# Gate, up and down of a feed-forward layer: the two products of neighbouring blocks in the order high, low, low, high

## The chip, the cores and the metric

The kernel runs on one core of a Trainium2 chip. The metric is the device time of one execution in microseconds (us), as the median of several runs. An execution under the hardware profiler gives the trace from which the rows in this document are copied.

## The reference

The program is the trunk of a streaming encoder: four layers on an input of 256 tokens by 1024 channels. Each layer has a token mixer (RWKV-7 time mixing in layers 0 and 3, stick-breaking attention in layer 1, attention over selected keys in layer 2) and a feed-forward part, each behind an RMS norm and with a residual add. The part that matters here is the feed-forward one:

```python
D_MODEL, SEQ, DEPTH = 1024, 256, 4
D_FF = -(-8 * D_MODEL // (3 * 256)) * 256      # 2816

def swiglu(h, w_gu, w_down):
    g, u = jnp.split(h @ w_gu, 2, axis=-1)
    return (jax.nn.silu(g) * u) @ w_down
...
        x = x + y
        x = x + swiglu(rms_norm(x, norm_ffn[i]), ffn_w_gu[i], ffn_w_down[i])
```

All is float32.

## The kernel before

**Data.** Channels lie on the 128 partitions, tokens along the free dimension. The residual stream is in four tiles `xt[j]`, each with two blocks of 128 channels by 256 tokens. A product needs a float32 result, but TensorE takes its operands in the format float32r at one pass. So each operand is split into a high part (the value rounded to float32r) and a low part (the value less the high part). A product of two split operands is made of three: high by high, high by low, low by high.

**The long and the short product.** For an activation block the high and the low part stand side by side in one tile, 512 columns. With the high weights loaded, one matmul over all 512 columns makes high by high in columns 0 to 255 of a PSUM bank and high by low in columns 256 to 511. With the low weights loaded, a second matmul over the first 256 columns adds low by high to columns 0 to 255. These two, called the high and the low product below, belong to one block of 128 input channels. Each needs its own weight load, a row LDWEIGHTS of engine PEld in the profile. The two halves of the bank are added later, by ScalarE's copy of columns 256 to 511 and VectorE's addition of columns 0 to 255 (`add2`, line 903).

**Weights.** `piece` (line 858) fetches 128x1024 float32 of weights by one DMA issued on SyncE into a tile `raw` (three buffers). The high part is made by a cast (`wh`, ScalarE as a rule), the low part by VectorE's subtraction (`wl`). There are three buffers of each. In gate and up every second piece uses three more pairs in the tile `wring`. A piece holds eight blocks of 128x128.

**Gate and up.** `ffn` (line 1019) runs over 11 groups of 256 channels. In each it makes two gate products and two up products by `gemm1` (line 908): eight blocks, each a unit of a high and a low product, summed in one bank. The moving tile is `xg`, the scaled input. ScalarE writes its high part block by block, VectorE its low part (`prep_chunk`, line 950). Then come scaling, SiLU, the product of gate and up, and the split of the result into `h`, high and low side by side. `gemm1` is also what layer 1's attention uses for its queries and keys (tile `qk`).

**Down.** For each of eight blocks of output channels, 22 blocks of `h` are summed in one bank `dn`, each again as a unit of a high and a low product; a piece covers eight blocks. VectorE then adds the bank to `xt`.

**What sets the order.** All operations are first recorded, and a planner (`Plan`) then orders them by a model of costs and due times, engine by engine. A unit (`with unit()`) is one entry for it: its matmuls stay together, in the order in which they were recorded. Units of different products may be mixed, save where `in_turn` keeps gate and up, or down, in their order. The instructions are all issued by one line of `emit`, so the profile shows nearly all of them as L779, and operations are told apart by their tiles.

**Other places of this trace that the prediction uses.** `vps` are layer 1's (and layer 2's) values: there the activations are loaded as weights, and the split weights move, 512 columns at a time, in the order high, low, high. `po` are the output projections, `qi` layer 2's index queries and `qk` layer 1's and 2's queries and keys. In `po`, `qi` and layer 2's `qk`, 256 columns move at a time, and the weights are in turn high, high, low. `warm_o` are products of constant data that keep TensorE busy.

Of the kernel before, what the change touches and what calls it, by code (L numbers as in the profile page):

```python
# [23 lines left out]
S = 256  # L24
D = 1024
NC = D // P
NF = 11
# [268 lines left out]
class Plan:  # L296
# [15 lines left out]
    def unit(self, at_once=1, ns=0.0):  # L312

        plan = self

        class Unit:
            def __enter__(self):
                plan.unit_op = Op("tensor")
                plan.unit_op.ns = ns

            def __exit__(self, *_):
                op, plan.unit_op = plan.unit_op, None
                op.cost /= at_once
                op.cost = op.ns or op.cost
                plan._add(op)

        return Unit()
# [63 lines left out]
    def after(self, op, preds):  # L391
        op.preds |= set(preds)
# [390 lines left out]
def trunk(ctx: ExitStack, tc: tile.TileContext, xT_in, vecs_in, wts, lora_in, consts_in, id32_in, outT, order, layers=None):  # L783
# [7 lines left out]
    pe, dve, act, pool, sp = (plan.queue(n) for n in ("tensor", "vector", "scalar", "gpsimd", "sync"))  # L791
# [3 lines left out]
    def T(shape, group=None, name="t", dtype=F32):  # L795
        return plan.tile(sb, [P] + list(shape), dtype, group, name)
# [7 lines left out]
    def bank(name, group="ps"):  # L804
        return plan.tile(psum, [P, 512], F32, group, name, "psum")
# [48 lines left out]
    def f(ap):  # L854
        return ap.bitcast(F32)


    def piece(key, raw=None, parts=None):

        i = len(order)  # L860
        order.append(key)
        r = T([PIECE], "raw", f"raw{i}") if raw is None else raw
        sp.dma_start(r, wts[i])
        h, l = (T([PIECE], "wh", f"wh{i}", F32R), T([PIECE], "wl", f"wl{i}", F32R)) if parts is None else parts
        anye.copy(h, r)
        dve.tensor_tensor(l, r, f(h), op=ALU.subtract)
        return h, l
# [26 lines left out]
    def v3(t, n):  # L894
        return t.rearrange("p (k m) -> p k m", k=n)
# [4 lines left out]
    def flat(t):  # L900
        return t.rearrange("p a b -> p (a b)")

    def add2(t, o, eng=anye):

        eng.copy(t, o[:, S:])
        dve.tensor_tensor(t, o[:, :S], t, op=ALU.add)

    def gemm1(key, x, name, group="g", raw=None, parts=None):


        out = bank(name, group)
        wh, wl = [v3(t, NC) for t in piece(key, raw, parts)]
        for c in range(NC):
            with unit():
                pe.matmul(out, wh[:, c], flat(x[:, c]), start=(c == 0), stop=False)
                pe.matmul(out[:, :S], wl[:, c], x[:, c, 0], start=False, stop=(c == NC - 1))
        return out

    def gemm2(key, xs, name):
# [76 lines left out]
    def rstd_bcast(summed=False):  # L996
        if summed:
            ss = nstate["ss"]
        else:
            ss, sq = bank("ss"), t1("ssq")  # L1000
            anye.tensor_tensor(sq, nstate["acc"][:, 0], nstate["acc"][:, 1], op=ALU.add)
            exact(ss[:, :S], onesr, sq, [T([S], "t", "ssr", F32R) for _ in range(2)])
        return rsqrt_of(ss[:, :S], S, "rstd", 1.0 / D, eps_rms)
# [15 lines left out]
    def ffn(layer, after):  # L1019
        x = nstate["xg"]  # L1020
        rsb = None
        hs = [v.rearrange("p (i k a s) -> p i k a s", i=n, k=2, a=2)
              for v, n in ((T([4096], g, "h", F32R), 4) for g in ("SA", "SZ", "PR"))]

        ring = T([6, PIECE], "QC", "wring", F32R)

        def place(n):

            return {"parts": (ring[:, n // 2 % 3], ring[:, 3 + n // 2 % 3]) if n % 2 else None}

        for i in range(NF):
            gus = T([2, 2, S], f"s{6 + i % 2}", "gus")
            gs, us = gus[:, 0], gus[:, 1]
            since = len(plan.ops)
            for k in range(2):
                add2(gs[:, k], gemm1(("g", layer, 2 * i + k), x, "gate", **place(4 * i + k)), act if i >= 0 else anye)
            if i == 0:
                rsb = rstd_bcast()[:, None, :].to_broadcast([P, 2, S])
            dve.tensor_tensor(gs, gs, rsb, op=ALU.mult)
            act.activation(gs, gs, AF.Silu)  # L1040
            for k in range(2):
                add2(us[:, k], gemm1(("u", layer, 2 * i + k), x, "up", "ps", **place(4 * i + 2 + k)), act if i >= 0 else anye)
            if i >= 1:
                plan.in_turn(since, "gate", "up")
            dve.tensor_tensor(us, us, rsb, op=ALU.mult)
            dve.tensor_tensor(us, us, gs, op=ALU.mult)
            h = hs[i // 4][:, i % 4]
            act.copy(h[:, :, 0], us)
            dve.tensor_tensor(h[:, :, 1], us, f(h[:, :, 0]), op=ALU.subtract)

        n, since = 0, len(plan.ops)
        for m in range(NC):
            o = bank("dn", "g" if m % 2 else "ps")
            for k in range(2 * NF):
                if n % NC == 0:
                    wh, wl = [v3(t, NC) for t in piece(("d", layer, n // NC))]
                h = hs[k // 8][:, k // 2 % 4, k % 2]
                with unit():
                    pe.matmul(o, wh[:, n % NC], flat(h), start=(k == 0), stop=False)
                    pe.matmul(o[:, :S], wl[:, n % NC], h[:, 0], start=False, stop=(k == 2 * NF - 1))  # L1060
                n += 1
            for a in range(2):
                dve.tensor_tensor(xt[m // 2][:, m % 2], xt[m // 2][:, m % 2], o[:, a * S:(a + 1) * S], op=ALU.add)
            if m == NC - 1:
                plan.in_turn(since, "dn")
            if m % 2:
                after(m // 2)
# [500 lines left out]
    def stick(layer, after):  # L1568
# [12 lines left out]
        for p in range(8):  # L1581
            q, k = qk_[:, p, 0], qk_[:, p, 1]
            add2(q, gemm1(("sq", p), x, "qk"))
            add2(k, gemm1(("sk", p), x, "qk"))
            if p == 0:
# [377 lines left out]
```

## Time and profile before

| | us |
|---|---|
| median of 3 runs | 1396.13 |
| lowest and highest of these | 1396.02, 1396.16 |
| the profiled execution | 1397.01 |
| its span, first to last instruction | 1395.1 |

In layer 0 the feed-forward part's gate and up run from 193.6 to 318.7 us of the span, and its down from there to 379.7.

In the profile PE is TensorE's matmuls, PEld its weight loads, DVE VectorE, ACT ScalarE, POOL GpSimd and SP SyncE. A group's row has the line, the engine, the operation, output and input tiles, the shapes and the count; then the busy time in us and the mean of one in ns; then the time for which the engine was idle ahead of them, and what ended it. A row in order of time has the start in us, the length in us from the first start to the last end, and then the same names. Rows of equal names that follow each other are merged, with their count. A row of a stretch has the stretch, its length, TensorE's busy time with the count of instructions, the granted clock, the share of DMA and GB/s. Ends of matmuls are modelled, and a record is longer than the time for which it holds the engine.

### The profile page before, as it was taken

The numbers are of one execution on the slowest core, as the hardware profiler recorded it, in microseconds if no ns is written. First come the engines' busy times: TensorE is split into PE (matmuls) and PEld (weight loads), VectorE is DVE, ScalarE is ACT, GpSimd is POOL, SyncE is SP. The second block draws the span as 40 slices with busy tenths as digits, with TensorE's granted clock in tenths as the row PEclk, the third lists the DMA queues.
The fourth block names the chain that finished last, engine by engine and source line by source line (L and its number), as shares of the span: only waits on it lengthen the run. The fifth ranks groups of instructions, "written<-read, shape, count | busy, mean of one in ns | idle before, by whom it ended". The sixth has DMA issues, their size and how long they took to land.

```text
span 1395.1 us, 25701 instructions
## 1 busy us (share of the span) xinstructions
PE 1376.2 (99%) x10404; PEld 1184.4 (85%) x10404; DVE 1076.0 (77%) x1791; ACT 802.8 (58%) x1362; POOL 7.6 (1%) x16
## 2 busy tenths in 40 slices
PE   9999999999999999999999999999999999999998
PEld 6887888888888888888988788888878877888887
DVE  7998498876676788876668988876579985888754
ACT  3765576654456676554545876654438465766532
POOL 0000000000000000000000000000000000000000
PEclk9999999999999999999999999999999999999999
DMA  6423056665654357646654336766635220567654
GB/s 225 145 91 122 19 168 205 204 178 164 191 168 150 107 180 214 203 145 194 195 167 132 95 107 212 219 190 209 187 91 170 91 92 18 168 203 209 176 172 128
DMA packets 61317, 219.84 MB, mean 158 GB/s; under 512 B 6800, under 2 KB 8080, under 8 KB 60944
## 3 DMA queue, kind: packets, MB, share of 16 engines
q1 hardware_dynamic: 61200, 218.22, 50.8%
q8 instruction: 81, 1.33, 0.4%
q14 instruction: 36, 0.29, 0.1%
HBM read 217.14 MB, written 1.05 MB: 156 GB/s over the span
## 4 chain that ended last, share of the span: by engine, by line
PE 79%; DVE 12%; DMA 4%; ACT 3%; issue 2%; DVEq 0%; ACTq 0%
PE dn L779 17%; PE up L779 14%; PE gate L779 14%; PE qk L779 6%; DMA raw<-in_wts_dram 4%; PE rp L779 3%; PE kp L779 3%; PE po L779 3%; PE vps L779 3%; PE z L779 2%; DVE wl L779 2%; DVE inv L779 2%; DVE xtmp L779 1%; PE sc L779 1%; PE attn_o L779 1%
## 5 line engine op out<-in xcount | busy, mean ns | idle before, releaser
L779 DVE TENSOR_TENSOR wl<-raw,wh 128x1024 fp32r<-128x1024 f32 x285 | 347.9, 1223 | 142.0 <-ACT wh L779 140.2
L779 ACT CAST wh<-raw 128x1024 fp32r<-128x1024 f32 x268 | 280.8, 1049 | 234.0 <-PE dn L779 99.7
L779 PE MATMUL dn<-h,wh 128*128 128x512 f32 x704 | 244.2, 390 | 0.0
L779 PE MATMUL dn<-h,wl 128*128 128x256 f32 x704 | 198.5, 282 | 0.0
L779 PEld LDWEIGHTS dn<-h,wh 128*128 128x128 f32 x704 | 132.2, 188 | 27.7
L779 PE MATMUL gate<-xg,wring 128*128 128x512 f32 x704 | 133.0, 337 | 4.0 <-DVE wring L779 3.1
L779 PEld LDWEIGHTS dn<-h,wl 128*128 128x128 f32 x704 | 133.0, 189 | 0.0
L779 PE MATMUL up<-xg,wring 128*128 128x512 f32 x704 | 132.4, 336 | 0.0
L779 PEld LDWEIGHTS gate<-xg,wring 128*128 128x128 f32 x704 | 107.4, 188 | 22.0 <-DVE wring L779 5.4
L779 PE MATMUL gate<-xg,wh 128*128 128x512 f32 x352 | 125.5, 395 | 0.2
L779 PE MATMUL up<-xg,wh 128*128 128x512 f32 x352 | 125.1, 392 | 0.0
L779 DVE TENSOR_TENSOR wring<-raw,wring 128x1024 fp32r<-128x1024 f32 x88 | 107.4, 1221 | 17.3 <-ACT wring L779 16.4
L779 PEld LDWEIGHTS up<-xg,wring 128*128 128x128 f32 x704 | 107.4, 188 | 14.4
L779 ACT CAST wring<-raw 128x1024 fp32r<-128x1024 f32 x87 | 91.5, 1052 | 33.8 <-DMA raw<-in_wts_dram 25.8
L779 PE MATMUL up<-xg,wl 128*128 128x256 f32 x352 | 98.5, 280 | 0.0
L779 PE MATMUL gate<-xg,wl 128*128 128x256 f32 x352 | 98.4, 280 | 0.0
L779 PE MATMUL qk<-xg,wh 128*128 128x256 f32 (+1 forms) x384 | 96.7, 332 | 0.0
L779 PEld LDWEIGHTS gate<-xg,wh 128*128 128x128 f32 x352 | 66.0, 188 | 16.6 <-DVE xg L779 1.3
L779 PEld LDWEIGHTS up<-xg,wh 128*128 128x128 f32 x352 | 66.1, 188 | 14.5
L779 PEld LDWEIGHTS qk<-xg,wh 128*128 128x128 f32 x384 | 64.0, 188 | 9.7 <-issue 4.2
L779 PE MATMUL qk<-xg,wl 128*128 128x256 f32 x256 | 71.7, 280 | 0.0
L779 PEld LDWEIGHTS up<-xg,wl 128*128 128x128 f32 x352 | 66.1, 188 | 0.2
(306 smaller groups left out, 2592.9 us busy)
## 6 DMA issues: line engine op xcount, KB each, us to landing
raw<-in_wts_dram SPq DMA_DIRECT2D x397, 512.0 KB, 3.7
lora<-in_lora_dram SPq DMA_DIRECT2D x2, 1536.0 KB, 9.9
xt<-in_xT_dram SPq DMA_DIRECT2D x4, 256.0 KB, 3.7
lora<-in_lora_dram SPq DMA_DIRECT2D x2, 512.0 KB, 6.1
lg<-in_lora_dram SPq DMA_DIRECT2D x8, 128.0 KB, 3.9
inv<-in_id_dram SPq DMA_DIRECT2D x2, 512.0 KB, 3.7
out_dram<-xt SPq DMA_DIRECT2D x4, 256.0 KB, 3.6
lg<-in_lora_dram SPq DMA_DIRECT2D x2, 256.0 KB, 3.6
```

The costliest lines, as they stand in the source:

```text
L779: getattr(getattr(nc, o.eng), method)(*map(real, args), **{k: real(a) for k, a in kw.items()})
```

## The change

In `gemm1` and in the down loop of `ffn`, blocks of even number keep the order high product, low product. Blocks of odd number have the low one first. The mark of the last product of a sum goes to the high product, which is now the last.

```diff
         for c in range(NC):
             with unit():
-                pe.matmul(out, wh[:, c], flat(x[:, c]), start=(c == 0), stop=False)
-                pe.matmul(out[:, :S], wl[:, c], x[:, c, 0], start=False, stop=(c == NC - 1))
+                for k in (0, 1) if c % 2 == 0 else (1, 0):
+                    if k == 0:
+                        pe.matmul(out, wh[:, c], flat(x[:, c]), start=(c == 0), stop=(c == NC - 1))
+                    else:
+                        pe.matmul(out[:, :S], wl[:, c], x[:, c, 0], start=False, stop=False)
...
                 with unit():
-                    pe.matmul(o, wh[:, n % NC], flat(h), start=(k == 0), stop=False)
-                    pe.matmul(o[:, :S], wl[:, n % NC], h[:, 0], start=False, stop=(k == 2 * NF - 1))
+                    for i in (0, 1) if k % 2 == 0 else (1, 0):
+                        if i == 0:
+                            pe.matmul(o, wh[:, n % NC], flat(h), start=(k == 0), stop=(k == 2 * NF - 1))
+                        else:
+                            pe.matmul(o[:, :S], wl[:, n % NC], h[:, 0], start=False, stop=False)
```

The following rows are TensorE's at the start of layer 0's down products, before. `dn` is the bank, `h` the moving tile, `wh` and `wl` the high and low weights of one piece; a row in brackets says on which engines' signals it waits.

```order
L779 MATMUL dn<-h,wh_3462 128x512 [waits Activation_49]
L779 MATMUL dn<-h,wl_3472 128x256 [waits DVE_49]
L779 MATMUL dn<-h,wh_3462 128x512
L779 MATMUL dn<-h,wl_3472 128x256
L779 MATMUL dn<-h,wh_3462 128x512
```

The same place of the changed program, up to the beginning of the next piece (x2: two in a row):

```order
L779 MATMUL dn<-h,wh_3462 128x512 [waits Activation_49]
L779 MATMUL dn<-h,wl_3472 128x256 [waits DVE_49]
L779 MATMUL dn<-h,wl_3472 128x256
L779 MATMUL dn<-h,wh_3462 128x512 x2
L779 MATMUL dn<-h,wl_3472 128x256 x2
L779 MATMUL dn<-h,wh_3462 128x512 x2
L779 MATMUL dn<-h,wl_3472 128x256 x2
L779 MATMUL dn<-h,wh_3462 128x512 x2
L779 MATMUL dn<-h,wl_3472 128x256 x2
L779 MATMUL dn<-h,wh_3462 128x512
L779 MATMUL dn<-h,wh_3511 128x512 [waits Activation_49]
L779 MATMUL dn<-h,wl_3524 128x256 [waits DVE_49]
```

The first pair of a piece and its waits stay where they were; behind it equal products stand in twos, and the last high product of a piece is followed by the first of the next.

The second place is the start of layer 0's gate products on TensorE, as a difference. There the units of two gate products (one with `wh` and `wl`, one with `wring`) are mixed, and the units wait for `xg`, whose high part comes from ScalarE (Activation) and whose low part from VectorE (DVE).

```order
 L779 MATMUL gate<-xg,wl_2359 128x256
-L779 MATMUL gate<-xg,wh_2340 128x512 [waits Activation_49]
-L779 MATMUL gate<-xg,wl_2359 128x256
+L779 MATMUL gate<-xg,wl_2359 128x256 [waits Activation_49]
+L779 MATMUL gate<-xg,wh_2340 128x512
 L779 MATMUL gate<-xg,wring 128x512 [waits DVE_49,Activation_49]
 L779 MATMUL gate<-xg,wring 128x256
 L779 MATMUL gate<-xg,wh_2340 128x512 [waits DVE_49]
 L779 MATMUL gate<-xg,wl_2359 128x256
+L779 MATMUL gate<-xg,wl_2359 128x256 [waits Activation_49]
 L779 MATMUL gate<-xg,wh_2340 128x512 [waits DVE_49]
-L779 MATMUL gate<-xg,wl_2359 128x256
```

In the odd blocks the low product now stands ahead of the high one, and waits for ScalarE's half of `xg` alone. The order of units is the same.

## The prediction

> **What bounds the kernel now.** I read the page first, from top to bottom.
>
> ```profile
> PE 1376.2 (99%) x10404; PEld 1184.4 (85%) x10404; DVE 1076.0 (77%) x1791; ACT 802.8 (58%) x1362; POOL 7.6 (1%) x16
> ...
> PEclk9999999999999999999999999999999999999999
> ...
> PE 79%; DVE 12%; DMA 4%; ACT 3%; issue 2%; DVEq 0%; ACTq 0%
> PE dn L779 17%; PE up L779 14%; PE gate L779 14%; PE qk L779 6%; DMA raw<-in_wts_dram 4%; PE rp L779 3%; PE kp L779 3%; PE po L779 3%; PE vps L779 3%; PE z L779 2%; DVE wl L779 2%; DVE inv L779 2%; DVE xtmp L779 1%; PE sc L779 1%; PE attn_o L779 1%
> ...
> L779 PE MATMUL dn<-h,wh 128*128 128x512 f32 x704 | 244.2, 390 | 0.0
> L779 PE MATMUL dn<-h,wl 128*128 128x256 f32 x704 | 198.5, 282 | 0.0
> ```
>
> TensorE is busy 99% of the span, at full granted clock throughout, and the chain that ended last runs 45% through dn, up and gate: exactly the products that the change reorders. The mean of 390 or 282 ns is the length of one record. Records overlap, so it is no price. What counts is the gap from one start to the next, and only the order of time shows that. The down stage of layer 0 begins and ends with these rows:
>
> ```profile
> 318.70 0.39 PE L779 MATMUL dn<-h,wh 128*128 128x512 f32 x1
> 318.93 0.28 PE L779 MATMUL dn<-h,wl 128*128 128x256 f32 x1
> 319.05 0.39 PE L779 MATMUL dn<-h,wh 128*128 128x512 f32 x1
> ...
> 379.72 0.40 PE L779 MATMUL qk<-xg,wh 128*128 128x512 f32 x1
> ```
>
> Call a 512-column high product a **long** and a 256-column low product a **short**. A long holds the engine 0.23 us and a short 0.12. More exactly, the stage's 176 pairs take 379.72 - 318.70 = 61.02 us, which is **346.7 ns a pair**, without a pause anywhere. Gate and up are the same pairs, but with a few pauses:
>
> ```profile
> 193.60:318.70 125.10, 123.63 (x708) 1.00 0.63 191
> 318.70:379.72 61.02, 61.02 (x355) 1.00 0.60 182
> ```
>
> Of 125.10 us of gate and up, TensorE is idle 1.5; of down, nothing. So whatever changes in the spacing of these matmuls goes straight into the time.
>
> **The change, part by part.** It adds and removes no instruction: 10404 matmuls stay 10404, and the order on VectorE, ScalarE, GpSimd and SyncE is the same row for row. Only TensorE's rows move. Long, short, long, short becomes long, short, short, long. The planner's unit is the pair, and its cost and dependences don't depend on what stands first in it.
>
> Counted in the order of the built programs: down has 352 places where a short now follows a short and 349 where a long follows a long. Gate and up have 680 and 676. The helper is also that of layer 1's query and key products, where there are 47 and 44. So the words of the change understate it a little. In all about 1073 times, a [long→short, short→long] is exchanged for a [short→short, long→long]. The whole question is what this exchange costs.
>
> First, what it can't change. A weight load begins as soon as the matmul ahead of it has begun:
>
> ```profile
> 302.06 0.39 PE L779 MATMUL up<-xg,wh 128*128 128x512 f32 x1
> 302.29 0.28 PE L779 MATMUL up<-xg,wl 128*128 128x256 f32 x1
> ```
>
> ```profile
> 302.07 0.19 PEld L779 LDWEIGHTS up<-xg,wl 128*128 128x128 f32 x1
> 302.30 0.19 PEld L779 LDWEIGHTS up<-xg,wh 128*128 128x128 f32 x1
> ```
>
> Each load therefore lies under one matmul. Before, half the loads lie under a long and half under a short, and after the change the halves are the same. If the load under a short is what costs, nothing is won by putting another short's load there.
>
> Second, what homogeneous streams cost. Both new neighbours stand elsewhere in the trace of before. Longs after longs are in vps (layer 1's values), where the weights move and the activations are loaded:
>
> ```profile
> 386.63 0.39 PE L779 MATMUL vps<-wl,xg 128*128 128x512 f32 x1
> 386.86 0.63 PE L779 MATMUL vps<-wh,xg 128*128 128x512 f32 x2
> 387.33 0.39 PE L779 MATMUL vps<-wl,xg 128*128 128x512 f32 x1
> ...
> 397.13 0.39 PE L779 MATMUL vps<-wl,xg 128*128 128x512 f32 x1
> ```
>
> The sequence is one low, two high, and from the first to the last of these rows it repeats 15 times: 45 gaps in 10.50 us, 233.3 ns each. Shorts after shorts are in po (the output projection) and, with the tile xg moving as in gate and up, in qi and qk of layer 2. Each again has one low and two high in turn:
>
> ```profile
> 484.27 0.28 PE L779 MATMUL po<-ohl,wl 128*128 128x256 f32 x1
> ...
> 495.82 0.28 PE L779 MATMUL po<-ohl,wl 128*128 128x256 f32 x1
> ```
>
> ```profile
> 682.04 0.28 PE L779 MATMUL qi<-xg,wl 128*128 128x256 f32 x1
> ...
> 688.16 0.28 PE L779 MATMUL qi<-xg,wl 128*128 128x256 f32 x1
> ```
>
> ```profile
> 717.15 0.28 PE L779 MATMUL qk<-xg,wl 128*128 128x256 f32 x1
> ...
> 728.06 0.28 PE L779 MATMUL qk<-xg,wl 128*128 128x256 f32 x1
> ```
>
> That is 33 rounds (99 gaps) in 11.55 us, or 116.7 ns; 17 rounds (51 gaps) in 6.12 us, or 120.0 ns; 31 rounds (93 gaps) in 10.91 us, or 117.3 ns.
>
> So a long and a short from unmixed streams cost 233.3 + 116.7 = 350.0 ns, and the alternating pair only 346.7. **Alternation is the cheaper form, by 3.3 ns a pair.** The trace doesn't say why. I take the saving to belong to the alternation, so that each exchange gives it up.
>
> With the po price for down: 350 x 3.3 ns = 1.2 us. With xg moving I take the qk price, the same tile in the longer stream: 233.3 + 117.3 - 346.7 = 3.9 ns, and 723 x 3.9 = 2.8 us. Together **+4.0 us**.
>
> The bounds of one exchange: at most 235 (the two gaps from 386.86 to 387.33, halved) + 120 - 346.7 = 8.3 ns, or +8.9 us. At least, if a long kept its 230 and a short after a short fell to the gap of the bfloat16 warm-up products, which have the same 256 columns:
>
> ```profile
> 8.89 3.33 PE L1797 MATMUL warm_o<-warm_x 128*128 128x256 bf16 x29
> ```
>
> These have 28 gaps in 3.33 less one record of 0.27, or 109 ns each. 230 + 109 - 346.7 is about -8 ns, or -8 us. The nearest rows are the float32 ones, so I stay with +4.0.
>
> [...]
>
> **Waits that move.** At the start of each feed-forward layer the first gate units wait for xg chunk by chunk:
>
> ```profile
> L779 PEld LDWEIGHTS gate<-xg,wh 128*128 128x128 f32 x352 | 66.0, 188 | 16.6 <-DVE xg L779 1.3
> ```
>
> In an odd chunk the long waits for VectorE's low half of xg, while the short needs only ScalarE's high half. With the short ahead, its 0.12 us runs inside that wait, once or twice a layer: at most 4 x 0.24 us; I take -0.3. Later in the same layer a gate long runs ahead of its low weights:
>
> ```profile
> 220.84 0.49 PE L779 MATMUL gate<-xg,wring 128*128 128x512 f32 x1 [0.55 <-ACT wring L779]
> 222.10 1.08 PE L779 MATMUL gate<-xg,wring 128*128 128x256 f32 x5 [0.77 <-DVE wring L779]
> ```
>
> Such a wait takes in a little of a slower stream ahead of it: some 25 us from the layer's start, about 35 exchanges of 3.9 ns, 0.14 us, in at most four layers; I take -0.2 in all.
>
> In the last pair of a product the long now ends 0.12 us later and the short 0.23 us earlier, while the pair as a whole ends at the same time (0.23 + 0.28 against 0.12 + 0.39). ScalarE's copy of the upper half, which only the long writes, may begin 0.12 us later, and the high weights' buffer is freed 0.12 us later. ScalarE waits there already:
>
> ```profile
> ACT wh L779 <- PE dn L779: 99.7, 60, 1.7
> ...
> ACT gus L779 <- PE gate L779: 41.9, 38, 1.6
> ```
>
> It is busy 58% of the span, and a cast (about 1.05 us) plus VectorE's subtraction (1.2) after a late release are covered by the two pieces, of eight pairs or 2.8 us each, that the other two buffers hold. I cost this at nothing. If that cover failed, the down stages' 88 pieces at 0.12 us would be +10 us. The idle time of dn's own rows, 0.0, speaks against.
>
> Sum: 4.0 - 0.3 - 0.2 = **+3.5 us**. The profiled execution took 1397.01 us (span 1395.1 and 1.9 around it), so it would be 1400.5. The median of the three runs is 0.9 lower, 1396.13, so I forecast **1399.6**.
>
> **Rivals.**
> *Own length only.* A matmul's gap depends on its own columns, and the 233.3 of vps comes from moving weights instead of activations. Then a long keeps 230 and a short 116.7, the exchange costs 346.7 against 346.7, and the time stays 1396.1. For: the short's 0.12 in the alternating rows equals po's. Against: po's and vps's gaps stand in exactly the ratio of their columns, 116.7 to 233.3, though their operands change roles, so the unmixed rate looks general. A second form has the same time: the saving belongs to two products over one chunk, and these stay neighbours. 26%.
> *The whole saving goes.* If it needs a short with longs on both sides, no pair keeps it. Then the price is twice 3.3, and qi's 120.0 instead of 117.3 may be added for xg: 1073 x 6.7 = +7.2, so 1403.3. 8%.
> *Changing length is what costs* (the other side, faster). The alternating pair pays 346.7 where two and one of the bfloat16 gaps of 109, 327 together, would do for the same columns. If the 20 ns over that were paid at the two changes of length, 10 each, then four matmuls in the new order have two changes instead of four: -20 ns x 1073 = -21 us, so 1375. It decides as soon as an unmixed stream is cheaper than the mixed one, and po, qi, qk and vps say the opposite, so the full size gets 3%. A smaller gain, from short loads that follow each other in one weight tile or from more than I allow at the layers' starts, some -4 us or 1392, gets 11%.
> *The change doesn't do what it says.* The order shows the new sequence in all three products, so there is nothing left of this.
>
> **How the numbers follow.** My forecast's case has 52%. Its sum crosses 0.2% (2.8 us, about what a measurement of this kernel can tell from no change) in four of five of its readings: 42% slower, 10% same. With the 8% of the whole saving, slower is 50%; with the 26% of own length, same is 36%; faster is 14%. The range goes from 1394.5, which leaves out most of the faster cases, to 1403.5, which takes in the whole saving and lies a little under the upper bound of +8.9 (1405).
>
> **What would show it.** Right: in the down stage of layer 0, 352 matmuls in 61.3 us instead of 61.02, hence 696.7 ns for four; short→short about 117, long→long about 233 where long→short stays about 229. Wrong: 61.02 again (own length), or four matmuls below 693 ns (length changes). ScalarE's waits for gate should be within a few us of before, and dn's rows should still have no idle time ahead of them. If those grow, the buffers' later release is what I missed.

## The result, and the profile after

| | us | ratio to the kernel before (95% interval) |
|---|---|---|
| before, median of 6 runs | 1396.08 | |
| changed, median of 6 runs | 1402.88 | 1.0054 (1.0040 to 1.0067) |
| profiled executions (span) | 1397.01 (1395.1), then 1402.87 (1401.1) | |

The changed kernel is **slower by 6.8 us**, 0.54%, where 3.5 was forecast. The direction was right, and the time lies inside the range, but the size is about twice the forecast. The page of the changed kernel, on TensorE and the chain:

```profile
PE 1381.2 (99%) x10404; PEld 1184.0 (85%) x10404; DVE 1076.8 (77%) x1791; ACT 802.2 (57%) x1362; POOL 11.7 (1%) x16
...
PEclk9999999999999999999999999999999999999999
...
PE dn L779 17%; PE up L779 15%; PE gate L779 14%; PE qk L779 6%; DMA raw<-in_wts_dram 3%; PE po L779 3%; PE rp L779 3%; PE kp L779 3%; PE vps L779 3%; PE z L779 2%; PE vp L779 2%; DVE wl L779 2%; PE sc L779 1%; DVE inv L779 1%; DVE xtmp L779 1%
...
L779 PE MATMUL dn<-h,wh 128*128 128x512 f32 x704 | 218.5, 391 | 0.0
L779 PE MATMUL dn<-h,wl 128*128 128x256 f32 x704 | 140.3, 281 | 0.0
```

The same 10404 matmuls, the clock still full (1.000 granted), the same order of costs. The busy sums of dn fell from 244.2 and 198.5 only because equal records now overlap each other; the gaps have to be read in order of time. In down of layer 0, changed kernel:

```profile
320.69 0.40 PE L779 MATMUL dn<-h,wh 128*128 128x512 f32 x1
...
339.89 0.62 PE L779 MATMUL dn<-h,wh 128*128 128x512 f32 x2
340.35 0.40 PE L779 MATMUL dn<-h,wl 128*128 128x256 f32 x2
340.58 0.62 PE L779 MATMUL dn<-h,wh 128*128 128x512 f32 x2
...
381.72 0.40 PE L779 MATMUL qk<-xg,wh 128*128 128x512 f32 x1
```

From 320.69 to 381.72 are 61.03 us, where it was 61.02. Call two longs and two shorts a **four**: the stage's 88 fours take 693.3 ns each, as before. **Down lost nothing.** Gate, in order of time:

```profile
298.42 0.40 PE L779 MATMUL gate<-xg,wl 128*128 128x256 f32 x2
298.66 0.63 PE L779 MATMUL gate<-xg,wh 128*128 128x512 f32 x2
299.12 0.40 PE L779 MATMUL gate<-xg,wl 128*128 128x256 f32 x2
...
299.83 0.40 PE L779 MATMUL gate<-xg,wl 128*128 128x256 f32 x2
```

From 298.42 to 299.83 are two fours in 1.41 us; over the long steady stretches, 703.3 ns each. **Gate and up lost 10 ns a four**, two and a half times the 3.9 forecast. The stretches from the first gate product to the first of down in the four layers (length, and time in which TensorE was busy), before and then changed, add up to:

```profile
sum 498.48, PE 494.30; mean PE 123.58
```

```profile
sum 502.77, PE 499.27; mean PE 124.82
```

So gate and up are 4.3 us longer in the profiles (3.7 in a second profile of the changed kernel, e5 below), with idle time down from 4.18 to 3.50. Layer 1's attention, which shares the helper, went from 116.29 to 116.70 us. These 4.7 us are all that the reordered stages show. Another 1.3 of the span's 6.0 lie ahead of the first reordered product (it starts at 194.98 instead of 193.65) and can't be the order's: a kernel of the old order (e3 below) started there at 194.57, and the changed one in a second profile at 194.48. The medians' difference of 6.8 us (interval 5.6 to 9.4) thus holds about 2 us that the reordered stages don't show.

The question is therefore not why two shorts in a row are dear. It is why the same order costs 10 ns a four over the tile xg and nothing over the tile h. The experiments below set theories against each other; each theory's letter is explained in the expectation where it first stands.

### The profile page after: what moved, and what is told of

The parts are those of the page before. It is cut to its first block, busy times and chain, and to the rows that moved or that the text cites. A ratio compares the mean times of both kernels' runs of the same rounds, so it can differ in the third digit from the quotient of the medians.

```text
span 1401.1 us, 25731 instructions
## 1 busy us (share of the span) xinstructions
PE 1381.2 (99%) x10404; PEld 1184.0 (85%) x10404; DVE 1076.8 (77%) x1791; ACT 802.2 (57%) x1362; POOL 11.7 (1%) x16
## 4 chain that ended last, share of the span: by engine, by line
PE 83%; DVE 9%; DMA 4%; ACT 2%; issue 1%; SPq 0%; DVEq 0%; ACTq 0%
PE dn L779 17%; PE up L779 15%; PE gate L779 14%; PE qk L779 6%; DMA raw<-in_wts_dram 3%; PE po L779 3%; PE rp L779 3%; PE kp L779 3%; PE vps L779 3%; PE z L779 2%; PE vp L779 2%; DVE wl L779 2%; PE sc L779 1%; DVE inv L779 1%; DVE xtmp L779 1%
## 5 line engine op out<-in xcount | busy, mean ns | idle before, releaser
L779 ACT CAST wh<-raw 128x1024 fp32r<-128x1024 f32 x268 | 280.8, 1049 | 241.8 <-PE dn L779 103.7
L779 PE MATMUL dn<-h,wh 128*128 128x512 f32 x704 | 218.5, 391 | 0.0
L779 PE MATMUL dn<-h,wl 128*128 128x256 f32 x704 | 140.3, 281 | 0.0
L779 PE MATMUL up<-xg,wring 128*128 128x512 f32 (+1 forms) x704 | 134.1, 338 | 0.0
L779 PE MATMUL gate<-xg,wh 128*128 128x512 f32 x352 | 119.7, 397 | 0.1
L779 PEld LDWEIGHTS dn<-h,wh 128*128 128x128 f32 x704 | 108.3, 188 | 0.0
L779 PEld LDWEIGHTS gate<-xg,wl 128*128 128x128 f32 x352 | 66.0, 188 | 15.3
L779 PE MATMUL up<-xg,wl 128*128 128x256 f32 x352 | 72.3, 281 | 0.0
L779 PE MATMUL gate<-xg,wl 128*128 128x256 f32 x352 | 70.2, 281 | 0.0
L779 PE MATMUL qk<-xg,wl 128*128 128x256 f32 x256 | 64.5, 282 | 0.0
L779 DVE TENSOR_TENSOR gus<-gus,rstd 128x512 f32<-128x512 f32 x88 | 60.8, 691 | 2.5
```

Of the source, the lines that this page charges most:

```text
L779: getattr(getattr(nc, o.eng), method)(*map(real, args), **{k: real(a) for k, a in kw.items()})
```

## The experiments

In the built programs, the weights' buffers (`wh`, `wl`, `wring`) begin at a multiple of 256 bytes in SBUF, xg at 17056 (160 past one) and the three h tiles at 82720, 99104 and 131872 (32 past one). HL is the alternating order, HLLH the changed one. A **place** is the first byte modulo 256. Rates for four matmuls are taken from start times in the steady part of a stream. A row that gives a count of matmuls in a stretch counts one or two that began earlier, too.

### e1: streams alone

Only streams of 64 matmuls, each over one tile, with the moving tile's place moved in steps of 32 bytes:

```diff
+ORDERS = {"hl": "HLHL", "hllh": "HLLH", "hh": "HHHH", "ll": "LLLL"}
+PLAN = [(o, m, 0) for m in range(0, 256, 32) for o in ORDERS]
+PLAN += [(o, m, w) for m in (32, 160) for w in (64, 128) for o in ("hl", "hllh")]
...
+                wv = wt[:, w // 4 + 1024 * half + P * c:w // 4 + 1024 * half + P * (c + 1)]
+                n_ = 512 if k == "H" else 256
+                nc.tensor.matmul(b[:, :n_], wv, mt[:, q + 512 * c:q + 512 * c + n_],
```

> This kernel leaves the reference's computation out and runs only streams of high (512 columns) and low (256 columns) products on one float32r tile: long/short alternating (HL), long short short long (HLLH), longs alone, shorts alone, with the moving tile's first column at 0, 32, ... 224 bytes past a multiple of 256, plus a few with the weights moved by 64 or 128. Theory A (place: what the order costs depends on where the moving tile begins within 256 bytes; xg begins at 160, the three h tiles at 32): four matmuls of HLLH take about 703 ns at 160 and 693 at 32, HL takes 693 at both. Theory B (region: xg lies in a low part of SBUF, h in a high one, and the place within 256 bytes is nothing): HLLH takes the same at all eight offsets. Theory C (company: the casts, the DMAs and the other stage's traffic beside gate and up cost the 10 ns): 693 for HLLH at every offset, since nothing runs beside these streams. My prediction's own theory (unmixed neighbours give up 3.3 ns a pair): HLLH is 696.7 everywhere and longs plus shorts alone 350.

Each stream is one row: its start, its length, its bank. HL at 0, HL and HLLH at 32, HL and HLLH at 64, HL and HLLH at 160, in this order:

```profile
19.39 11.45 PE L54 MATMUL pa<-x,w 128*128 128x512 f32 x64
...
64.05 11.26 PE L54 MATMUL pe<-x,w 128*128 128x512 f32 x64
75.15 11.26 PE L54 MATMUL pf<-x,w 128*128 128x512 f32 x64
...
108.72 11.45 PE L54 MATMUL pa<-x,w 128*128 128x512 f32 x64
120.01 11.22 PE L54 MATMUL pb<-x,w 128*128 128x512 f32 x64
...
243.20 11.26 PE L54 MATMUL pe<-x,w 128*128 128x512 f32 x64
254.30 11.40 PE L54 MATMUL pf<-x,w 128*128 128x512 f32 x64
```

With nothing beside them, the streams give the kernel's numbers: HL and HLLH at 32 both 11.26 us, at 160 11.26 against 11.40. Sixteen fours differ by 0.14 us; in the steady part it is 10 ns a four, 693.3 against 703.3, which is what down and gate show. Theory C (company) falls. So does theory B (region), for one tile in one region gave HLLH several rates, and so does the forecast's own: HLLH is not 696.7 everywhere. And **neither order is the cheaper one as such**. By place, in ns for four:

| place | 0 | 32 | 64 | 96 | 128 | 160 | 192 | 224 |
|---|---|---|---|---|---|---|---|---|
| HL | 706.7 | 693.3 | 706.7 | 700.0 | 702.2 | 693.3 | 706.7 | 693.3 |
| HLLH | 696.7 | 693.3 | 690.0 | 700.0 | 696.7 | 703.3 | 693.3 | 702.7 |

At 0, 64 and 192 the changed order wins 10 to 17 ns.

### e2, e3: xg laid at 32

```diff
-FIRST = ("xb_0", "wh_0", "wh_1", "wh_2", "wl_0", "wl_1", "wl_2", "QC_0", "SZ_0", "PR_0", "s0_0", "s1_0", "SA_0")
+FIRST = ("wh_0", "wh_1", "wh_2", "wl_0", "wl_1", "wl_2", "QC_0", "SZ_0", "xb_0", "PR_0", "s0_0", "s1_0", "SA_0")
-LINE = 128
-LEAD = {"xb_0": 32, "wh_0": 0, "SZ_0": 32}
+LINE = 256
+LEAD = {"wh_0": 128, "SZ_0": 160, "xb_0": 160}
```

`xb_0` is xg, and `SZ_0` is one of the h tiles. The leads count from the beginning of the stretch of SBUF that holds these tiles, 128 past a multiple of 256: a lead of 128 is the place 0, and 160 the place 32. e2 has the changed order, e3 the old one.

> The changed kernel with the tile xg laid between two of the h tiles, so that it begins at 32 bytes past a multiple of 256 as they do, and not at 160; the weights' buffers keep 0, and all else keeps its address or moves by a multiple of 4096. Theories A and B: gate and up fall from 703.3 to 693.3 ns for four matmuls, 7 us, so about 1396 us, the time before the change. Theory C: 703.3 stays, 1403 us.

> The kernel before with the same new place of xg: does the place alone, without the order, move the time? Theories A and B: the alternating order costs 346.7 ns a pair at either place, so 1396 us; layer 2's low-column streams over xg (qi, qk, 117 to 120 ns a gap) may fall to 116.7, at most 1 us. Theory C: the same, 1396.

e3 came out as expected, 1396.19 us, 0.9985 (0.9973 to 0.9997); layer 2's qi and qk did fall to 116.7 ns a gap. e2 didn't: **1408.29 us, 1.0068** (1.0049 to 1.0087), where theories A and B had about 1396. (Two of its ten executions took 1401.4 and 1402.3, the others 1406.7 to 1410.2; only one of these others has a trace.) The matmuls in a steady stretch of gate and up, and of down, of layer 0 (before, then e2):

```profile
235.00:315.00 80.00, 80.00 (x463) 1.00 0.66 198
325.00:375.00 50.00, 50.00 (x290) 1.00 0.63 190
```

```profile
235.00:315.00 80.00, 80.00 (x454) 1.00 0.64 192
325.00:375.00 50.00, 50.00 (x285) 1.00 0.60 181
```

Both stages run at 706.7 ns a four, which is not theory C's 703.3 either, and down as well, though the places of its h tiles are still 32. So a place has more than one rate.

### e4: the places exchanged

The h tiles first in SBUF at 160, xg behind at 32, by another order of `FIRST` and other leads.

> The changed kernel with the places exchanged: the three h tiles lie in the low part of SBUF and begin at 160 past a multiple of 256, xg lies high and begins at 32. Theories A and B: gate and up fall to 693.3 ns for four matmuls (-7 us), down rises from 693.3 to 703.3 (352 fours, +3.5 us): about 1399.5 us. Theory C: 703.3 stays in gate and up, 693.3 in down, 1403 us. If the down stage stays at 693.3 while gate and up fall, the place of the moving tile isn't the whole cause.

1409.29 us, 1.0076 (1.0051 to 1.0101). Down went up as theory A said, to 703.3 in three layers, but to 706.7 in layer 0: the place 160 has a second rate as well. Gate and up in layers 0 to 3:

```profile
235.00:315.00 80.00, 80.00 (x463) 1.00 0.66 197
...
540.00:615.00 75.00, 75.00 (x426) 1.00 0.66 201
...
875.00:950.00 75.00, 75.00 (x426) 1.00 0.69 203
...
1250.00:1325.00 75.00, 75.00 (x426) 1.00 0.69 208
```

Layer 0 is at 693.3 (463 in 80 us, as before); the others, with 426 in 75 us where before had 435, are at 706.7. Same program, same addresses, **two rates at the place 32**.

### e5 and e6: the same again, and other starts

e5 is the changed kernel again. e6 repeats streams of 48 at the same addresses, with one small matmul of another width ahead:

```diff
+        if shift:
+            nc.tensor.matmul(banks[7][:, :shift], wt[:, :P], mt[:, :shift], start=True, stop=True)
```

> The changed kernel once more, another execution. Theory D (the rate of a stream is set by the addresses of its tiles alone): gate and up at 703 ns for four matmuls and down at 693.3 in all four layers, as in the first profile. Theory E (a stream has several steady rates at the same addresses, and the moment at which it begins picks one): in some stage another rate between 690 and 707.

> This kernel leaves the reference's computation out. It runs 60 streams of 48 matmuls: alternating order (HL) or long short short long (HLLH), over three moving tiles 16640 bytes apart, at 32 or 160 past a multiple of 256, each at five starts that differ by one small matmul of 0, 8, 24, 40 or 72 columns ahead. A row's length is twelve fours and 0.16 us: 8.48 us is 693.3 ns for four, 8.60 is 703.3, 8.64 is 706.7. Theory D: the five starts of a cell have the same length. Theory E: they differ within a cell by up to 0.16 us, in either order.

e5 repeated the first profile in all eight stages (span 1400.0 us). In e6, HL at 32 and at 160 took 693.3 from each of five starts, and HLLH at 160 took 703.3 from each; the three tiles, 16640 bytes apart, were alike. HLLH at 32, from the five starts:

```profile
71.58 8.51 PE L54 MATMUL pf<-xa,w 128*128 128x512 f32 x48
...
80.43 8.58 PE L54 MATMUL pg<-xa,w 128*128 128x512 f32 x48
...
89.34 8.58 PE L54 MATMUL pa<-xa,w 128*128 128x512 f32 x48
...
98.25 8.58 PE L54 MATMUL pb<-xa,w 128*128 128x512 f32 x48
...
107.17 8.72 PE L54 MATMUL pc<-xa,w 128*128 128x512 f32 x48
```

In their steady part the first four run at 693.3, the last at 706.7, on all three tiles. (The first row is shorter only at its beginning, having no small matmul ahead.) So D and E each hold in part: **the place sets which rates a stream can have, and where there is more than one the start picks**. That fits e2 and e4: xg at 32 in the order HLLH landed on 706.7 in most stages. Down's 693.3 in the changed kernel was luck of its start.

### e7: a finer scan

> This kernel leaves the reference's computation out. It runs HL and HLLH at 32 places of the moving tile, 0, 8, ... 248 bytes past a multiple of 256, weights at 0; 48 matmuls each. Theory D: the rate is a function of the place, the same for 32 and 160 as in the first streams (HL 693.3 at both, HLLH 693.3 and 703.3). Theory E: it scatters between about 690 and 707 in both orders, without a rule by the place.

At 32 and 160 the rates were again 693.3 and 693.3, 693.3 and 703.3. Over all 32 places in steps of 8 bytes HL took 693.3 to 720.0 and HLLH 690.0 to 713.3, with no rule that I can read; 690.0 at 64 was the lowest. HL at 224 took 706.7 here and 693.3 in e1, so the old order has two rates at that place.

### e8: the old order at a bad place

> The kernel before, in the alternating order, with xg at a multiple of 256 and the h tiles still at 32 past one. In the first streams the alternating order took 706.7 ns for four at that place. Theory D: gate and up (704 fours) go from 693.3 to 706.7, +9.4 us, 1405.5 us: the alternating order has slow places too, and the kernel before was only laid out on a fast one. Theory E: a rate between 693.3 and 706.7, perhaps not the same in all layers; 1396 to 1405.5 us. If the alternating order in the full kernel is immune, 1396.

1400.86 us, 1.0014 (0.9998 to 1.0030), so by the time alone only a trend. The stages show it; gate and up of layers 0 to 3:

```profile
235.00:315.00 80.00, 80.00 (x455) 1.00 0.62 191
...
540.00:615.00 75.00, 75.00 (x426) 1.00 0.64 198
...
875.00:950.00 75.00, 75.00 (x435) 1.00 0.66 202
...
1250.00:1325.00 75.00, 75.00 (x426) 1.00 0.67 203
```

706.7 in layers 0, 1 and 3, and 693.3 in layer 2, a rate that no bare stream of HL at 0 showed. The alternating order isn't immune, and 0 has two rates for it as well. In this profile gate and up are 4.1 us longer than before, which is about what they lost in the changed kernel; the span is only 3.8 us longer.

### e9: both tiles moved

> This kernel leaves the reference's computation out. Streams of 48 matmuls, HL and HLLH, at eight pairs of places (moving tile, weights) within 256 bytes, four starts each: (0,0), (16,0), (64,0), (32,224), (144,0), (192,0), (160,128), (32,128); and low products alone (LL) at (32,0), (64,0), (160,0). Theory F: what counts is the difference of the two places modulo 256, so (64,0) and (32,224) behave alike, (160,128) as (32,0) did (HL 693.3, HLLH 693.3 or 706.7 by the start), and (32,128) as (160,0) did (HL 693.3, HLLH 703.3). Theory G: the moving tile's own place counts, whatever the weights': (32,224), (32,128) as (32,0), and (160,128) as (160,0). The fours of HLLH at (64,0) are 690.0 again if that place is fast from any start.

Rates in ns for four, from the four starts:

| moving, weights | difference | HL | HLLH |
|---|---|---|---|
| 64, 0 | 64 | 697.8, 706.7, 697.8, 706.7 | 690.0 (all) |
| 32, 224 | 64 | 706.7 (all) | 690.0 (all) |
| 160, 128 | 32 | 693.3 (all) | 693.3 (all) |
| 32, 128 | 160 | 693.3 (all) | 706.7, then 703.3 (three) |

Each of these is a rate that its difference gave with weights at 0 (706.7 at a difference of 160 in down of e4's layer 0). HLLH's 690.0 at (32,224), 693.3 at (160,128) and 703.3 at (32,128) are none of the rates that its moving place gave. The second starts of HL and HLLH at (64,0), then of both at (32,224), then of HLLH at (160,128) and at (32,128):

```profile
171.72 8.71 PE L56 MATMUL pd<-x,w 128*128 128x512 f32 x48
...
207.57 8.56 PE L56 MATMUL pa<-x,w 128*128 128x512 f32 x48
...
243.22 8.72 PE L56 MATMUL pe<-x,w 128*128 128x512 f32 x48
...
279.16 8.56 PE L56 MATMUL pb<-x,w 128*128 128x512 f32 x48
...
493.06 8.58 PE L56 MATMUL pe<-x,w 128*128 128x512 f32 x48
...
564.31 8.68 PE L56 MATMUL pf<-x,w 128*128 128x512 f32 x48
```

In e1, (160,64) gave 700.0 for both orders, as (96,0) did, and (32,64) gave 693.3 and 702.7, as (224,0) did. Theory F holds in the five pairs tried: **the difference of the two places counts**, for which rates occur. G falls. Which of them a start picks is not settled by the difference: the start with 72 columns gave HLLH 706.7 at (32,0) in e6 and 693.3 at (160,128) here. Low products alone have their rates, too: for four of them 466.7 ns at 32 from three starts and 471 from one, 471 at 64, and 469 at 160.

### e10, e11, e12: the changed order at a good place

e10 lays the weights at 224 and leaves xg and h at 32; e11 leaves the weights at 0 and lays xg and h at 64; e12 is e11's layout with the old order. The leads of e11 and e12 (128 is the place 0, 192 the place 64; `s0_0` is a tile of the output projections):

```diff
-LEAD = {"xb_0": 32, "wh_0": 0, "SZ_0": 32}
+LEAD = {"wh_0": 128, "s0_0": 160, "SZ_0": 192, "xb_0": 192}
```

> The changed kernel with the weights' buffers at 224 past a multiple of 256 and xg and h at 32, a difference of 64, the place at which HLLH took 690.0 ns in the first streams. Theory F: gate, up and down at 690.0 (one branch) or above; at 690 the three stages win 3.3 ns on each of 1056 fours, -3.5 us against the kernel before, but all other products over these weights change their difference too, and low products alone took 117.8 instead of 116.7 there, up to +3 us: 1393 to 1397. Theory G: the moving tile stays at 32, so 693.3 or 706.7 as in the second and first profile: 1396 or 1408.

> The changed kernel with weights at 0 and xg and h at 64 past a multiple of 256 (the tiles of the output projection stay at 32). Theories F and G: 690.0 ns for four in gate, up and down if that place has one rate, -3.5 us against the kernel before, 1392.6 us; if it has a second rate at other starts, up to 706.7 and 1410.

> The kernel before, in the alternating order, in the layout of the run with xg and h at 64. Theory F, with the rates of the streams (HL at a difference of 64: 697.8 or 706.7 ns for four): gate, up and down lose 4.5 to 13.4 ns on each of 1056 fours, 4.7 to 14 us, so 1401 to 1411 us. If the layout alone is what won in the run with xg and h at 64, this kernel would be as fast as that one, about 1393 us.

| difference of places | old order, HL | new order, HLLH |
|---|---|---|
| 160 for xg, 32 for h | 1396.08 | 1402.88, 1.0054 (1.0040 to 1.0067) |
| 64 for both | e12: 1407.10, 1.0068 (1.0046 to 1.0090) | e11: **1393.98, 0.9973 (0.9957 to 0.9989)** |

e10 took 1395.11 us, 0.9980 (0.9965 to 0.9995). Each ratio is against the kernel before on the same chip: 1398.6 us for e10 and e11, 1397.33 for e12. The steady stretches of e11, layer 0, then of gate and up in e12's four layers:

```profile
235.00:315.00 80.00, 80.00 (x466) 1.00 0.64 201
325.00:375.00 50.00, 50.00 (x291) 1.00 0.61 190
```

```profile
235.00:315.00 80.00, 80.00 (x454) 1.00 0.64 192
...
540.00:615.00 75.00, 75.00 (x431) 1.00 0.69 206
...
875.00:950.00 75.00, 75.00 (x426) 1.00 0.67 202
...
1250.00:1325.00 75.00, 75.00 (x427) 1.00 0.67 203
```

In their steady stretches e11 and e10 run at 690.0 in gate, up and down of every layer; e12 at 706.7, and in layer 1 at 697.8. This layout alone loses 0.7%, the order alone loses 0.5%, and both together win 0.3%: e11 beats the kernel before on its own chip, and by the ratios the changed one. It isn't shown to beat every layout of the old order: e3 had 0.9985 (0.9973 to 0.9997), and the intervals overlap, though e3's fours take 693.3.

## Why the prediction was wrong in size

The sums come out as written; what they were made of was wrong. That the direction was right and the time inside the range was luck of the layout and of the starts: at a difference of 64 the same change is faster (e12 to e11), and with the stages at their other rate the changed order is slower than the range allows (e2).

1. *What bounds the kernel.* Right: the time followed the spacing of these matmuls, from 0.9973 of the kernel before at 690.0 ns for four (e11) to 1.0068 at 706.7 (e2).
2. *Nothing is added, and the number of loads under a short stays.* The count is right. That the load's cover is therefore without effect was argued, and no run took a load away.
3. *The price of an exchange.* **This is the step that failed.** "I take the saving to belong to the alternation, so that each exchange gives it up": it doesn't belong to the alternation. In its place e1, e9 and e11 showed that the difference of the places of moving tile and weights sets the rates of either order (at 64, 690.0 ns for HLLH against 697.8 or 706.7 for HL), and e6 that the start picks among them (693.3 or 706.7 for HLLH at 32). Down's term was +1.2 us and measured 0: its 61.03 us is the sign that the prediction had named against itself. Gap by gap in layer 0 of the changed kernel, long to long took 226.7 ns in down and not 233.3. In gate and up it took 232.8, but there long to short, priced at an unchanged 229, took 234.5. Gate, up and the shared queries and keys were +2.8 and measured 4.3 + 0.4 = 4.7 in the profiles, at 10 ns a four instead of 3.9. The rates of vps and qk, which I added up with po's, were rates of those tiles' places (po's I didn't read at another place). With xg laid at 32 (e3), qk's 117.3 ns a gap fell to 116.7; with xg laid at 0 (e8), vps's 45 gaps took 227.3 ns each where I had read 233.3:

```profile
387.40 0.39 PE L779 MATMUL vps<-wl,xg 128*128 128x512 f32 x1
...
397.63 0.39 PE L779 MATMUL vps<-wl,xg 128*128 128x512 f32 x1
```

po's 116.7 and qk's 117.3 were even a warning: the same shapes at two rates with full clock and no wait. I read it as a spread of the operand xg and not as a quantity to be explained. qi shows two rates at one place, before any change: 120.0 in the 17 rounds that I read, and 117.2 in the 13 that follow behind two other matmuls (39 gaps in 4.57 us):

```profile
688.76 0.28 PE L779 MATMUL qi<-xg,wl 128*128 128x256 f32 x1
...
693.33 0.28 PE L779 MATMUL qi<-xg,wl 128*128 128x256 f32 x1
```

e1 shows how little such sums are worth: at 0 unmixed longs and shorts took 906.7 and 480.0 for four, so 346.7 for one of each, where HL there took 353.3 a pair and HLLH 348.3.
4. *The waits that move.* Forecast at -0.5; TensorE's idle time in gate and up fell by 0.7. At 10 ns, the 139 fours or so behind layer 0's last early wait (222 to 320 us) would give 1.4 us a layer, 5.6 in four; gate and up grew by 4.3, so the layers' starts took back rather more than I said.
5. *Late buffers and copies cost nothing.* Right: dn's rows have no idle time ahead of them, and ScalarE's longest wait, for dn, went from 99.7 to only 103.7 us.
6. *The rivals.* "Own length only" described down, and "the whole saving goes" has about the measured time (1403.3) for a reason that the streams refute. No rival named the layout, which decides the sign. The lower bound of one exchange, -8 ns, which I set aside for "the float32 rows", has the size of what the exchange wins at a difference of 64 (8 to 17 ns in the streams), though the short products there did not fall to the 109 ns from which it was made (short to short took 113 to 120 in gate and up of e11).

## What to carry to other kernels

When a stream of matmuls on a full TensorE shows the same shapes at two rates in one trace (here 703.3 in gate and up and 693.3 in down), compare the SBUF addresses of weights and moving tile modulo 256 before reasoning from the order. Time an order of matmuls at several places of its tiles, and from several starts: a change of order and a change of layout tested one at a time can each lose and win together. A small kernel of bare streams gave the full kernel's 693.3 and 703.3 to a nanosecond and cost half a millisecond on the chip; it didn't show every rate that a place has (e8's 693.3 at 0).

## What the hardware showed that I had not expected

- The rate of a gapless stream of float32r products depends on the difference, modulo 256 bytes, between the places of the moving tile and of the weights (five pairs in e1 and e9): 690.0 to 713.3 ns for two of 512 and two of 256 columns in the order HLLH, 693.3 to 720.0 in HL (e7).
- At some differences a stream has two steady rates and keeps the one into which it settles: 693.3 and 706.7 at 32 in the order HLLH, from starts that differ by one matmul of 72 columns (e6); in e4 gate and up held 693.3 in layer 0 and 706.7 in the three others over stretches of 75 or 80 us.
- Why is open. The weights' place counts as much as the moving tile's: HLLH took 690.0 with the moving tile at 64 and the weights at 0 and with the two at 32 and 224 (e9). How the one acts on the other was not shown: no run had such a stream without its loads, so whether the loads cost anything is open, too. What e9 does show is that the columns alone don't set the gap: the same columns took 690.0 to 706.7.
